# An MLP in two phases with its activations spilled to DRAM, and the up projection of most pairs of feature blocks with seven products for eight

## The chip, the cores and the metric

The kernel runs on one core of a Trainium2 chip. The metric is the time of one execution on the device in microseconds (us).

## The reference

One step of a one-layer decoder: an RWKV-7 branch and an mLSTM branch run on the same projection, are merged by gates, go through an output projection and then a squared-ReLU MLP. Two sets of tokens, 1024 of a prompt (with 16 meta tokens ahead) and 8 x 8 of running sequences, share the weights; after the mixing stages 1088 token columns are left. The change touches the end of the merge, the output projection and the MLP:

```
merged = ga * (ya @ p_a) + gb * (yb @ p_b)
h = x + rms_norm(merged @ w_out, post1)
u2 = rms_norm(h, pre2)
f = square(relu(u2 @ w_ff_up)) @ w_ff_down      # 1024 -> 4096 -> 1024
out = h + rms_norm(f, post2)
```

## The kernel before

All large products are made in float32 accuracy from three matmuls: an operand is split into a high part (`hi`, rounded) and a low part (`lo`, the rest), and `gemm` issues hi x hi, hi x lo and lo x hi into one PSUM bank (lines L219, L220, L221). Weights are loaded by `wload`: one DMA of 512 KB on SyncE's queue (L195), a cast on ScalarE (`hi`, L200) and subtractions on GpSimd (`lo`, L207) or VectorE (L203). Each of two pools (`wps`) holds one raw tile and two pairs of split ones, so weights come about one group ahead.

The merge (L1555 to L1568) makes `mg`, the 1088 token columns for 8 blocks of 128 rows, high and low part: for each of the 8 blocks it loads a row of gates (`gb`) and of the other branch (`pa`), multiplies on TensorE with p_b, and combines on VectorE (L1564), GpSimd (L1565), ScalarE (L1566) and VectorE (L1567). `wo_gemm` then multiplies with w_out, 8 blocks of 128 tokens and a ninth of 64 (the samples); for the ninth, high and low part stand side by side in one 128-column operand (`mgt`), two matmuls for three, except at k = 6. `pre_turn` transposes the normed result (L1606) back into `mg` (L1609, L1610).

The MLP works in 15 groups of f, blocks of 128 of the 4096 hidden features: three f, 13 times two, three f. For each group `up` makes the hidden rows of each f: three token tiles (`O_TILES`: 384, 384 and 320 columns) x 8 blocks k x 3 matmuls, then Relu (ScalarE, L1710), square (VectorE, L1711), cast (ScalarE, L1712) and subtraction (VectorE, L1716) into `AHS[f % 3]`. `down` then multiplies, for each of 8 blocks of tokens and both halves of the 1024 outputs, 3 matmuls of 512 columns per f, adds the bank to `ACC` on VectorE (L1771), and `down_tail` (L1735) does the ninth block. Up and down alternate, so only two or three f of hidden rows exist at a time, in SBUF. The first group's up is woven with the last three transposes (`todo`); the last group's down part is woven with the final norm and the outputs by hand (`manual_schedule`); elsewhere a scheduler sets the order of each engine's instructions from the program.

Of the kernel before, what the change touches and what calls it, by code (L numbers as in the profile page):

```python
# [8 lines left out]
F32 = mybir.dt.float32  # L9
# [8 lines left out]
D = 1024  # L18
# [84 lines left out]
def tile_hybrid_trunk_step(ctx, tc, x_prompt, x_sample, st_S, st_shift, st_C, st_n, st_m, st_conv,  # L103
# [58 lines left out]
    NKK = cp.tile([128, 4], F32, name="NKK")  # L162
    OKA = cp.tile([128, 4], F32, name="OKA")
# [1389 lines left out]
    for m in range(8):  # L1553
# [7 lines left out]
        for a, n in O_TILES:  # L1561
# [37 lines left out]
    def pre_turn(i, un_):  # L1599
        n, un = BL[i][1], un_.pop(i)  # L1600
        ts_ = slice(128 * i, 128 * i + n)
        for h in range(2):
# [5 lines left out]
            uh = mg[:, 0, 4 * h:4 * h + 4, ts_]  # L1608
            nc.scalar.copy(out=uh, in_=pv)  # L1609
            V.tensor_tensor(out=mg[:, 1, 4 * h:4 * h + 4, ts_], in0=pv, in1=uh.bitcast(F32), op=ALU.subtract)  # L1610
# [251 lines left out]
```

## Time and profile before

| | |
|---|---|
| median of 3 runs | 2058.99 us (2058.14 to 2061.21) |
| profiled execution | 2053.6 us, of which the span of the trace 2051.8 us |
| granted TensorE clock over the span | 0.987 of full speed |
| TensorE busy | 1943.2 us (95%), 12,325 matmuls in the trace |
| weight loads (PEld) | 1762.7 us (86%) |
| VectorE, ScalarE, GpSimd busy | 1266.4 (62%), 729.1 (36%), 589.4 us (29%) |
| DMA | 161.63 MB, 24.6% of the 16 engines' span |

A busy share is an average over stages with different limits; the MLP takes the last 790 of the 2052 us. Matmuls are pipelined: their durations overlap, and what one costs is the distance from its start to the next start.

### The profile page before, as it was taken

What the parts mean: (1) busy time and instruction counts of PE and PEld (TensorE: products, weight loads), DVE (VectorE), ACT (ScalarE), POOL (GpSimd) and SP (SyncE); (2) the same over time, 40 slices, a digit from 0 to 9 for tenths busy, and PEclk for the clock granted to TensorE, in tenths of its full rate; (3) what the DMA queues carried; (4) which work ended last, traced back from release to release, by engine and by line L of the source; (5) the groups of instructions that cost most, each with busy time, mean ns of one, the idle gap of its engine ahead of it and who ended that gap; (6) DMA issues with size and microseconds to landing.
All of it is one profiled execution on the core that took longest, in us unless ns stands there. A gap on an engine that the chain in (4) does not pass through costs nothing.

```text
span 2051.8 us, 32757 instructions
## 1 busy us (share of the span) xinstructions
PE 1943.2 (95%) x12325; PEld 1762.7 (86%) x12325; DVE 1266.4 (62%) x3527; ACT 729.1 (36%) x1706; POOL 589.4 (29%) x937
## 2 busy tenths in 40 slices
PE   8999899999999999999899998999999999999996
PEld 8988788888888888989788777889999999988895
DVE  6378778867877887777765469244444444444447
ACT  6444344433443343546554234322222222211122
POOL 3321221322122121353435115133222322232225
PEclk9999999999999999999999999999999999999998
DMA  5222112112111221143756334111111111111114
GB/s 157 56 77 66 47 56 64 58 47 67 63 56 56 67 66 57 54 129 117 233 185 206 132 99 153 32 52 42 52 52 42 42 51 43 42 42 52 42 37 163
DMA packets 148495, 161.63 MB, mean 79 GB/s; under 512 B 20428, under 2 KB 121606, under 8 KB 148336
## 3 DMA queue, kind: packets, MB, share of 16 engines
q1 hardware_dynamic: 148336, 159.54, 24.6%
q8 instruction: 97, 1.59, 0.3%
q14 instruction: 62, 0.51, 0.1%
HBM read 121.98 MB, written 37.27 MB: 78 GB/s over the span
## 4 chain that ended last, share of the span: by engine, by line
PE 63%; DVE 22%; DMA 7%; issue 3%; ACT 2%; POOL 1%; SPq 0%; DVEq 0%; ACTq 0%; POOLq 0%
PE g L219 11%; PE g L221 11%; PE g L220 11%; PE g L287 5%; PE g L283 5%; PE g L285 5%; DMA NR<-ndr 3%; DVE tmp L773 2%; DVE x L775 2%; DMA ndr<-nd 1%; PE g L1735 1%; DVE Vs L909 1%; PE a L713 1%; PE g L1635 1%; PE g L1637 1%
## 5 line engine op out<-in xcount | busy, mean ns | idle before, releaser
L207 POOL TENSOR_TENSOR lo<-raw,hi 128x128 fp32r<-128x128 f32 (+1 forms) x736 | 414.7, 596 | 985.8 <-ACT hi L200 971.6
L283 PE MATMUL g<-u,hi 128*128 128x414 f32 (+4 forms) x1120 | 379.8, 339 | 1.5 <-ACT hi L200 0.8
L287 PE MATMUL g<-u,lo 128*128 128x414 f32 (+4 forms) x1120 | 381.0, 340 | 0.0
L285 PE MATMUL g<-u,hi 128*128 128x414 f32 (+4 forms) x1120 | 378.9, 338 | 0.0
L200 ACT CAST hi<-raw 128x1024 fp32r<-128x1024 f32 x124 | 128.6, 1048 | 379.3 <-PE g L1735 275.8
L219 PE MATMUL g<-mg,hi 128*128 128x384 f32 (+1 forms) x768 | 251.7, 328 | 0.6 <-ACT mg L1609 0.6
L220 PE MATMUL g<-mg,hi 128*128 128x384 f32 (+1 forms) x768 | 251.4, 327 | 0.3 <-DVE mg L1610 0.3
L221 PE MATMUL g<-mg,lo 128*128 128x384 f32 (+1 forms) x768 | 251.5, 328 | 0.0
L1771 DVE TENSOR_TENSOR ACC<-g,ACC 128x512 f32<-128x512 f32 x234 | 161.4, 690 | 129.5 <-PE g L221 123.4
L283 PEld LDWEIGHTS g<-u,hi 128*128 128x128 f32 x1120 | 214.1, 191 | 6.8 <-issue 1.5
L287 PEld LDWEIGHTS g<-u,lo 128*128 128x128 f32 x1120 | 213.8, 191 | 4.9 <-POOL lo L207 0.3
L285 PEld LDWEIGHTS g<-u,hi 128*128 128x128 f32 x1120 | 213.7, 191 | 3.7 <-issue 0.2
L219 PE MATMUL g<-hi,ah 128*128 128x512 f32 (+1 forms) x515 | 202.9, 394 | 0.0
L220 PE MATMUL g<-lo,ah 128*128 128x512 f32 (+1 forms) x515 | 202.7, 394 | 0.0
L221 PE MATMUL g<-hi,ah 128*128 128x512 f32 (+1 forms) x515 | 202.4, 393 | 0.0
L219 PEld LDWEIGHTS g<-mg,hi 128*128 128x128 f32 x768 | 144.1, 188 | 1.5 <-ACT mg L1609 0.9
L220 PEld LDWEIGHTS g<-mg,hi 128*128 128x128 f32 x768 | 144.2, 188 | 1.2 <-DVE mg L1610 0.5
L221 PEld LDWEIGHTS g<-mg,lo 128*128 128x128 f32 x768 | 144.2, 188 | 0.0
L221 PEld LDWEIGHTS g<-hi,ah 128*128 128x128 f32 x515 | 96.7, 188 | 22.9
L219 PEld LDWEIGHTS g<-hi,ah 128*128 128x128 f32 x515 | 96.6, 187 | 22.3
L220 PEld LDWEIGHTS g<-lo,ah 128*128 128x128 f32 x515 | 96.7, 188 | 22.0
L773 DVE TENSOR_TENSOR tmp<-NR,x 128x45 f32<-128x45 f32 (+4 forms) x360 | 82.5, 229 | 28.4 <-DMA NR<-ndr 21.1
(855 smaller groups left out, 3482.1 us busy)
## 6 DMA issues: line engine op xcount, KB each, us to landing
raw<-in_w_in_dram SPq DMA_DIRECT2D x44, 512.0 KB
raw<-in_w_ff_up_dram SPq DMA_DIRECT2D x32, 512.0 KB
raw<-in_w_ff_down_dram SPq DMA_DIRECT2D x32, 512.0 KB
NR<-ndr SPq DMA_DIRECT2D x24, 384.0 KB
gscr<-gst SPq DMA_DIRECT2D x16, 544.0 KB
xt<-in_x_prompt_dram SPq DMA_DIRECT2D x15, 512.0 KB
ga<-gscr SPq DMA_DIRECT2D x8, 544.0 KB
pscr<-ga SPq DMA_DIRECT2D x8, 544.0 KB
```

Of the source, the lines that this page charges most:

```text
L200: nc.scalar.copy(out=hi, in_=raw)
L207: PO.tensor_tensor(out=lo[:, k:k + step], in0=raw[:, k:k + step], in1=hi[:, k:k + step].bitcast(F32), op=ALU.subtract)
L219: mm(ps, lhsT=wh, rhs=xh, start=(i == 0), stop=False)
L220: mm(ps, lhsT=wh, rhs=xl, start=False, stop=False)
L221: mm(ps, lhsT=wl, rhs=xh, start=False, stop=(i == last))
L283: mm(ps, lhsT=hi[:, k], rhs=xh, start=(k == 0), stop=False)
L285: mm(ps, lhsT=hi[:, k], rhs=xl, start=False, stop=False)
L287: mm(ps, lhsT=lo[:, k], rhs=xh, start=False, stop=(k == 7))
L713: mm(ps[:, 192 * (c - c0):192 * (c - c0) + 192], lhsT=flat(bd["a"][:, c]), rhs=flat(KB[:, c]), start=True, stop=True)
L773: V.tensor_tensor(out=tmp[:, :, :n], in0=NR[:, s + 1:16, :, s].rearrange("p t c -> p c t"), in1=x[:, :, s:s + 1].broadcast_to([128, G, n]) ...
L775: V.tensor_tensor(out=x[:, :, s + 1:16], in0=x[:, :, s + 1:16], in1=tmp[:, :, :n], op=ALU.add)
L1771: V.tensor_tensor(out=ACC[:, i, cs], in0=ps, in1=ACC[:, i, cs], op=ALU.add)
```

## The change

The hidden rows no longer stay in SBUF: phase 1 makes all 32 f and writes them to DRAM tensors `hD[f]`, phase 2 reads them back (`h_load`: DMA, cast, subtraction, four casts of the 32 sample columns each) into four buffers `AHS[f % 4]` and runs `down` as before.

In phase 1 the f 0 to 5 (`NCONV`) are made as before, with the square on ScalarE. The other 26 are 13 pairs. For a pair the product is seen as 2 x 2 blocks: the two f, the two halves of the 1024 inputs (4 blocks k each), and two interleaved halves of the tokens; Strassen's form (with shared sums) makes seven products in place of eight. A product is 2 quarters of the tokens (`q`) x 4 k x 3 matmuls of 272 columns. Products 1, 2 and 3 read `mg` itself, where the 272 columns are two runs of 136; products 5, 6, 7 and 4 read token sums T1 to T4, built once by `t_quads` on VectorE (28 operations of 128x1088) and ScalarE (8 casts). On the weight side `pair_prep` makes four sums S on VectorE and seven operands (cast on ScalarE, subtraction on GpSimd). `pair` puts the products together: two copies on ScalarE and 14 additions from PSUM on VectorE, then Relu and Square on ScalarE (128x1088, two of each) and four writes to `hD`.

So that a block of tokens has one size, `mg` is laid out in 8 blocks of 136 columns (128 of the prompt and 8 samples); the merge writes its last token tile in two pieces, and the ninth block of `wo_gemm` is stacked at k = 6 too. The seven products have eight PSUM banks instead of five. The last group's hand-written order is the same.

```diff
+            e = min(a + n, 1024)
+            parts = [(gb[:, a:e].rearrange("p (b c) -> p b c", c=128), [mgb[:, y, m, a // 128:e // 128, :128] for y in range(2)])]
+            if e < a + n:
+                parts.append((gb[:, 1024:].rearrange("p (b c) -> p b c", c=8), [mgb[:, y, m, :, 128:] for y in range(2)]))
+            for src, (mh, ml) in parts:
+                act(out=mh, in_=src, func=AF.Copy, scale=0.5)
+                V.scalar_tensor_tensor(out=ml, in0=src, scalar=0.5, in1=mh.bitcast(F32), op0=ALU.mult, op1=ALU.subtract)
...
-                    if i == 8 and k != 6:
-                        st_ = mgt[2][:, 0] if k == 4 else mgt[0][:, k] if k < 3 else mgt[1][:, k // 2 - 1]
+                    if i == 8:
+                        st_ = mgt[2][:, k // 2 - 2] if k in (4, 6) else mgt[0][:, k] if k < 3 else mgt[1][:, k // 2 - 1]
                         mm(ps, lhsT=st_, rhs=wh_, start=(k == 0), stop=False)
...
+    hD = [dp.tile([128, TO], F32, name=f"hD{f}") for f in range(32)]
+    HALF = [slice(0, 512), slice(512, 1024)]
+    NCONV = 6
+    PORDER = (1, 2, 6, 5, 7, 3, 4)
...
+            r_ = tmp()[:, :n]
+            act(out=r_, in_=ps, func=AF.Relu)
+            act(out=r_, in_=r_, func=AF.Square)
+            dma(out=hD[f][:, a:a + n], in_=r_)
...
+    for n in (4, 3, 1, 2):
+        phX[n] = ctx.enter_context(ExitStack())
+        T[n] = phX[n].enter_context(tc.tile_pool(name=f"tp{n}", bufs=1, side="right")).tile([128, 2, 4, TO // 2], F32R, name=f"T{n}")
...
+    def t_quads(q):
+        B = lambda j, l, y: mgb[:, y, 4 * j:4 * j + 4, 4 * q + l:4 * q + 4:2, :].bitcast(F32)
+        Tv = lambda n, y: T[n][:, y, :, HQ2 * q:HQ2 * q + HQ2].rearrange("p k (u c) -> p k u c", c=136)
+        fa, fb = [htile().rearrange("p k (u c) -> p k u c", c=136) for _ in range(2)]
+
+        def tt(o, x, y, op=ALU.subtract):
+            V.tensor_tensor(out=o, in0=x, in1=y, op=op)
+
+        def diff(b1, b2):
+            tt(fa, B(*b1, 0), B(*b2, 0))
+            tt(fb, B(*b1, 1), B(*b2, 1))
+            tt(fa, fa, fb, ALU.add)
+
+        def rest(o, b1, x):
+            tt(o, B(*b1, 0), x)
+            tt(o, o, B(*b1, 1), ALU.add)
+
+        def fin_(n, x):
+            nc.scalar.copy(out=Tv(n, 0), in_=x)
+            tt(Tv(n, 1), x, Tv(n, 0).bitcast(F32))
+
+        diff((0, 1), (0, 0))
+        rest(fb, (1, 1), fa)
+        fin_(1, fa)
+        rest(fa, (1, 0), fb)
+        fin_(2, fb)
+        fin_(4, fa)
+        diff((1, 1), (0, 1))
+        fin_(3, fa)
...
+    def operand(src):
+        o = slots[0]
+        slots[0] += 1
+        t_ = wps[o % 2].tile([128, 2, 4, 128], F32R, tag=("hi", "lo")[o // 2 % 2], name="op")
+        nc.scalar.copy(out=t_[:, 0], in_=src)
+        PO.tensor_tensor(out=t_[:, 1], in0=src, in1=t_[:, 0].bitcast(F32), op=ALU.subtract)
+        return t_
...
+    def pair_prep(p):
+        A = pair_load(p)
+        S = [stile() for _ in range(4)]
+        ops = {1: operand(A[0][0]), 2: operand(A[0][1])}
+        V.tensor_tensor(out=S[0], in0=A[1][0], in1=A[1][1], op=ALU.add)
+        V.tensor_tensor(out=S[1], in0=S[0], in1=A[0][0], op=ALU.subtract)
+        ops[6] = operand(S[1])
+        ops[5] = operand(S[0])
+        V.tensor_tensor(out=S[2], in0=A[0][0], in1=A[1][0], op=ALU.subtract)
+        ops[7] = operand(S[2])
+        V.tensor_tensor(out=S[3], in0=A[0][1], in1=S[1], op=ALU.subtract)
+        ops[3] = operand(S[3])
+        ops[4] = operand(A[1][1])
+        return ops
...
+    def Bop(n, y, k, q):
+        if n in (1, 2, 3):
+            j, l = ((0, 0), (1, 0), (1, 1))[n - 1]
+            return mgb[:, y, 4 * j + k, 4 * q + l:4 * q + 4:2, :]
+        return T[{5: 1, 6: 2, 7: 3, 4: 4}[n]][:, y, k, HQ2 * q:HQ2 * q + HQ2].rearrange("p (u c) -> p u c", c=136)
+
+    def prod(n, op, ps, q):
+        o = ps.rearrange("p (u c) -> p u c", c=136)
+        for k in range(4):
+            xh, xl = Bop(n, 0, k, q), Bop(n, 1, k, q)
+            mm(o, lhsT=op[:, 0, k], rhs=xh, start=(k == 0), stop=False)
+            mm(o, lhsT=op[:, 0, k], rhs=xl, start=False, stop=False)
+            mm(o, lhsT=op[:, 1, k], rhs=xh, start=False, stop=(k == 3))
+
+    def pair(p, ops):
+        X, H = {}, {}
+        add = lambda o, ps, x: V.tensor_tensor(out=o, in0=ps, in1=x, op=ALU.add)
+        for n in PORDER:
+            for q in range(2):
+                ps = gbank()[:, :HQ2]
+                prod(n, ops[n], ps, q)
+                if n == 1:
+                    X[q] = upp.tile([128, HQ2], F32, tag="X", name="X", bufs=4)
+                    H[q] = htile()
+                    nc.scalar.copy(out=X[q], in_=ps)
+                    continue
+                c11, c12, c21, c22 = [H[q][:, i] for i in range(4)]
+                if n == 2:
+                    add(c11, ps, X[q])
+                elif n == 6:
+                    add(X[q], ps, X[q])
+                elif n == 5:
+                    add(c12, ps, X[q])
+                elif n == 7:
+                    add(c22, ps, c12)
+                    add(c21, ps, X[q])
+                elif n == 3:
+                    add(c12, ps, c12)
+                elif n == 4:
+                    add(c21, ps, c21)
+                    act(out=H[q], in_=H[q], func=AF.Relu)
+                    act(out=H[q], in_=H[q], func=AF.Square)
+                    for i in range(2):
+                        dma(out=hD[2 * p + i][:, 2 * HQ2 * q:2 * HQ2 * q + 2 * HQ2], in_=H[q][:, 2 * i:2 * i + 2].rearrange("p s c -> p (s c)"))
+
+    for q in range(2):
+        t_quads(q)
+    for f in range(3, NCONV):
+        w, w3 = w3, up_load(f + 1) if f + 1 < NCONV else None
+        up(f, w, O_TILES, t1)
+    ops = pair_prep(NCONV // 2)
+    for p in range(NCONV // 2, 16):
+        nxt = pair_prep(p + 1) if p < 15 else None
+        pair(p, ops)
+        ops = nxt
...
+    hraw = lambda: dn.tile([128, TO], F32, tag="hr", name="hr", bufs=2)
+    AHS = [dn.tile([128, 2 * TO + 128], F32R, name=f"ah{i}") for i in range(4)]
...
+    def h_load(f):
+        ah, hr = AHS[f % 4], hraw()
+        dma(out=hr, in_=hD[f])
+        hi, lo, st_ = ah[:, :TO], ah[:, TO:2 * TO], ah[:, 2 * TO:]
+        nc.scalar.copy(out=hi, in_=hr)
+        V.tensor_tensor(out=lo, in0=hr, in1=hi.bitcast(F32), op=ALU.subtract)
+        for y, src in enumerate((hi, lo)):
+            for q in range(2):
+                v = src[:, 544 * q:544 * q + 544]
+                v = v.rearrange("p (u s c) -> p u s c", u=2, s=2) if f < NCONV else v.rearrange("p (s u c) -> p u s c", u=2, s=2)
+                nc.scalar.copy(out=st_[:, 64 * y + 32 * q:64 * y + 32 * q + 32].rearrange("p (u s c) -> p u s c", u=2, s=2),
+                               in_=v[:, :, :, 128:].bitcast(F32))
...
-    V.memset(SS, 1.0)
     for g, fs in enumerate(groups):
-        wu = [wload(kxm(w_ff_up[0], 128 * f, 128), 8, 128) for f in fs]
+        for f in fs:
+            h_load(f)
         if g == 0:
-            todo = [5,None,None,6,7]
```

On TensorE, a steady group of before passes from the up projection (`mg` against `hi`/`lo` of the weights) to the down projection (`ah` against the split down weights):

```order
L219 MATMUL g<-mg,hi 128x320
L220 MATMUL g<-mg,hi 128x320
L221 MATMUL g<-mg,lo 128x320
L219 MATMUL g<-hi,ah_13552 128x512
L220 MATMUL g<-lo,ah_13552 128x512
L221 MATMUL g<-hi,ah_13552 128x512
```

It is so in every group. After the change, a place in pair 10 (the second half of its 48 matmuls on `mg` for products 1 and 2 ends, product 6 on T2, `T_14800`, begins; `op` are the split weight operands, L1836 to L1838 the three matmuls):

```order
L1836 MATMUL g<-mg,op 128x272
L1837 MATMUL g<-mg,op 128x272
L1838 MATMUL g<-mg,op 128x272
L1836 MATMUL g<-T_14800,op 128x272 [waits DVE_49,Activation_49]
L1837 MATMUL g<-T_14800,op 128x272
L1838 MATMUL g<-T_14800,op 128x272 [waits Pool_49]
```

For each f stood 72 matmuls of 384 and 320 columns; for two f now stand 168 of 272, and no down projection stands between the pairs.

On SyncE's queue, where the loads of before alternate between up and down weights, a group ahead, at the change from phase 1 to phase 2 stand (`hD<-H` are writes of the last two pairs, `hr<-hD` the loads of f = 0, 1, 2, `raw` the down weights):

```order
L1869 DMA hD_14420<-H 128x544 [waits DMAHW5_49,Activation_49]
L1869 DMA hD_14421<-H 128x544 [waits DMAHW6_49,DVE_49]
L195 DMA raw<-in_w_ff_down_dram 128x1024 [waits DMAHW7_49,Activation_49,Pool_49]
L195 DMA raw<-in_w_ff_down_dram 128x1024 [waits DMAHW0_49,Pool_49]
L1899 DMA hr<-hD_14392 128x1088 [waits DMAHW1_49,PE_49]
L1899 DMA hr<-hD_14393 128x1088 [waits DMAHW2_49]
L195 DMA raw<-in_w_ff_down_dram 128x1024 [waits DMAHW3_49,DMAHW7_49,Activation_49,Pool_49]
L1899 DMA hr<-hD_14394 128x1088 [waits DMAHW4_49,DMAHW1_49,DVE_49]
L1869 DMA hD_14422<-H 128x544 [waits DMAHW5_49,Activation_49]
L1869 DMA hD_14423<-H 128x544 [waits DMAHW6_49]
L1869 DMA hD_14422<-H 128x544 [waits Activation_49]
L1869 DMA hD_14423<-H 128x544 [waits DMAHW0_49,DVE_49]
```

The loads of hidden rows are in the queue between weights and the last pair's writes; the first waits for TensorE, the third for VectorE.

On ScalarE at the same place (f = 0 is `ah_18289`, f = 1 `ah_18290`, f = 2 `ah_18291`; L1866 and L1867 are Relu and Square of pair 15):

```order
L1901 CAST ah_18289<-hr 128x1088 [waits DMAHW1_49]
L1866 ACTIVATE H<-H 128x1088 [waits DMAHW4_49,DMAHW3_49,DVE_49]
L1907 CAST ah_18289<-ah_18289 128x32 [waits Activation_49]
L1867 ACTIVATE H<-H 128x1088 [waits Activation_49]
L1866 ACTIVATE H<-H 128x1088 [waits DMAHW6_49,DMAHW5_49,DVE_49]
L1907 CAST ah_18289<-ah_18289 128x32
L1867 ACTIVATE H<-H 128x1088 [waits Activation_49]
L1907 CAST ah_18289<-ah_18289 128x32 x2
L1901 CAST ah_18290<-hr 128x1088 [waits DMAHW2_49]
L1901 CAST ah_18291<-hr 128x1088 [waits DMAHW4_49]
```

The cast of f = 0 stands ahead of pair 15's Relu and Square, those of f = 1 and 2 behind them.

On TensorE the last matmul of pair 15 is followed by 21 matmuls on f = 0, and these end so:

```order
L221 MATMUL g<-hi,ah_18289 128x512
L219 MATMUL g<-hi,ah_18290 128x512 [waits Activation_49]
L220 MATMUL g<-lo,ah_18290 128x512 [waits Pool_49]
L219 MATMUL g<-hi,ah_18290 128x512
L220 MATMUL g<-lo,ah_18290 128x512 [waits Pool_49]
L219 MATMUL g<-hi,ah_18290 128x512
L220 MATMUL g<-lo,ah_18290 128x512
L221 MATMUL g<-hi,ah_18290 128x512 [waits DVE_49]
L219 MATMUL g<-hi,ah_18291 128x512 [waits Activation_49]
```

Seven banks of group 0 are begun with f = 0 alone before f = 1 is asked for, and f = 2 is asked for 7 matmuls later.

## Rows read from the trace of the kernel before

**Rows 1.** Stretches: busy us of each engine (instructions), granted clock, DMA share, GB/s.

```profile
1260.00:1310.00 50.00, 48.12 (x279) 45.10 (x278) 32.51 (x64) 19.55 (x37) 18.79 (x23) 1.00 0.29 94
1400.00:1500.00 100.00, 100.00 (x520) 90.64 (x519) 41.40 (x67) 20.43 (x34) 27.08 (x45) 1.00 0.15 45
2000.00:2052.00 52.00, 33.68 (x155) 27.68 (x153) 41.02 (x77) 13.49 (x39) 28.20 (x20) 0.86 0.44 165
```

**Rows 2.** TensorE's waits, 1255 to 2052 us: total us, times, longest. Five rows.

```profile
PE s L1606 <- DVE SS L1589: 1.2, 1, 1.2
...
PE g L220 <- DVE mg L1610: 0.3, 1, 0.3
```

**Rows 3.** Timeline of TensorE, one steady group: start us, duration us.

```profile
1480.95 0.34 PE L219 MATMUL g<-mg,hi 128*128 128x384 f32 x1
1481.12 0.34 PE L220 MATMUL g<-mg,hi 128*128 128x384 f32 x1
...
1504.67 0.31 PE L221 MATMUL g<-mg,lo 128*128 128x320 f32 x1
1504.82 0.39 PE L219 MATMUL g<-hi,ah 128*128 128x512 f32 x1
...
1528.78 0.39 PE L1735 MATMUL g<-lo,ah 128*128 128x512 f32 x1
1529.01 0.34 PE L219 MATMUL g<-mg,hi 128*128 128x384 f32 x1
```

**Rows 4.** Timeline of TensorE: end of the first up part, last matmul.

```profile
1300.49 0.40 PE L219 MATMUL g<-hi,ah 128*128 128x512 f32 x1
...
2033.41 0.27 PE L221 MATMUL g<-hi,ah 128*128 128x192 f32 x1
```

**Rows 5.** Timeline of TensorE in the projection: two runs, 6 intervals of 276 columns each.

```profile
306.10 0.29 PE L283 MATMUL g<-u,hi 128*128 128x276 f32 x1
...
306.85 0.29 PE L283 MATMUL g<-u,hi 128*128 128x276 f32 x1
...
308.45 0.29 PE L287 MATMUL g<-u,lo 128*128 128x276 f32 x1
...
309.21 0.29 PE L287 MATMUL g<-u,lo 128*128 128x276 f32 x1
```

**Rows 6.** Groups by line and form: count, busy us, mean ns, idle before.

```profile
L219 PEld LDWEIGHTS g<-mg,hi 128*128 128x128 f32 x768 | 144.1, 188 | 1.5 <-ACT mg L1609 0.9
L1771 DVE TENSOR_TENSOR ACC<-g,ACC 128x512 f32<-128x512 f32 x234 | 161.4, 690 | 129.5 <-PE g L221 123.4 <-PE g L1735 6.1
L1564 DVE SCALAR_TENSOR_TENSOR gb<-gb,g 128x384 f32<-128x384 f32 x16 | 8.4, 546 | 4.4 <-DMA gb<-gscr 4.4
L207 POOL TENSOR_TENSOR lo<-raw,hi 128x128 fp32r<-128x128 f32 x672 | 332.1, 528 | 713.0 <-ACT hi L200 698.8 <-ACT R L252 11.6 <-issue 1.6
L207 POOL TENSOR_TENSOR lo<-raw,hi 128x512 fp32r<-128x512 f32 x64 | 82.7, 1316 | 272.8 <-ACT hi L200 272.8
L1609 ACT CAST mg<-s 128x512 fp32r<-128x512 f32 x16 | 8.8, 586 | 5.4 <-PE s L1606 5.4
L200 ACT CAST hi<-raw 128x1024 fp32r<-128x1024 f32 x124 | 128.6, 1048 | 379.3 <-PE g L1735 275.8 <-PE g L220 48.0 <-PE g L285 17.8
```

**Rows 7.** Timeline of GpSimd, then of VectorE, near 1295 us.

```profile
1294.68 2.80 POOL L207 TENSOR_TENSOR lo<-raw,hi 128x512 fp32r<-128x512 f32 x2 [20.16 <-ACT hi L200]
...
1294.91 1.41 DVE L1711 TENSOR_TENSOR r__14667<-r__14667 128x320 f32<-128x320 f32 x1 [2.51 <-ACT r__14667 L1710]
```

**Rows 8.** Single lines: duration min/median/max ns, first and last start us.

```profile
L1415 DVE TENSOR_TENSOR yh<-yt,yh x2: 1292/1292/1293, 1001.6 to 1074.9; 128x1088 fp32r<-128x1088 f32 x2
...
L1414 ACT CAST yh<-yt x3: 1087/1099/1100, 1000.5 to 1073.8; 128x1088 fp32r<-128x1088 f32 x3
...
L1610 DVE TENSOR_TENSOR mg<-s,mg x18: 411/682/690, 1222.6 to 1286.8; 128x512 fp32r<-128x512 f32 x16, 128x256 fp32r<-128x256 f32 x2
```

**Rows 9.** Chain that ended last, in the merge: start us, us, what.

```profile
1100.87 4.71 DMA gb<-gscr
```

More of the change, by code (lines that the diff above doesn't have):

```diff
@@ L1607, in pre_turn @@
             pv = pt.rearrange("p (k t) -> p k t", k=4)[:, :, :n]
-            uh = mg[:, 0, 4 * h:4 * h + 4, ts_]
+            ks = slice(4 * h, 4 * h + 4)
+            uh, ul = [mgb[:, y, ks, i, :128] if i < 8 else mgb[:, y, ks, :, 128:] for y in range(2)]
+            if i == 8:
+                pv = pv.rearrange("p k (b c) -> p k b c", c=8)
             nc.scalar.copy(out=uh, in_=pv)
-            V.tensor_tensor(out=mg[:, 1, 4 * h:4 * h + 4, ts_], in0=pv, in1=uh.bitcast(F32), op=ALU.subtract)
+            V.tensor_tensor(out=ul, in0=pv, in1=uh.bitcast(F32), op=ALU.subtract)
     SS = sm.tile([128, 11, 2], F32, tag="SS", name="SS", bufs=1)
@@ L1718, in tile_hybrid_trunk_step, with up_load @@
-    gam3 = gam1
-    dma(out=gam3, in_=post2.broadcast_to([128, D]))
-    HALF = [slice(0, 512), slice(512, 1024)]
+            r_ = tmp()[:, :n]
+            act(out=r_, in_=ps, func=AF.Relu)
+            act(out=r_, in_=r_, func=AF.Square)
+            dma(out=hD[f][:, a:a + n], in_=r_)
+    def up_load(f):
+        return wload(kxm(w_ff_up[0], 128 * f, 128), 8, 128)
+    t1 = lambda: rpool.tile([128, 384], F32, tag="r_", name="r_")
+    wu = [up_load(f) for f in range(3)]
+    todo = [5, None, None, 6, 7]
@@ new lines, in tile_hybrid_trunk_step @@
+    for tile_ in O_TILES[:2]:
+        for f, w in enumerate(wu):
+            up(f, w, (tile_,), t1)
+            for i in todo[:1]:
+                if i:
+                    pre_turn(i, un_)
+            todo = todo[1:]
+    w3 = up_load(3)
+    for f, w in enumerate(wu):
+        up(f, w, O_TILES[2:], t1)
+    phN.close()
+    phS.close()
+    gps3 = ctx.enter_context(tc.tile_pool(name="gps3", bufs=3, space=PSUM))
+    gpss[:] = (gps, gps2, gps3, gps2, gps3, gps, gps2, gps3)
+    phT = ctx.enter_context(ExitStack())
@@ new lines, in tile_hybrid_trunk_step, with pair_load @@
+    slots = [0]
+    def operand(src):
[5 more added lines that the diff above has]
+        return t_
+    def pair_load(p):
+        srcs = [kxm(w_ff_up[0], 256 * p + 128 * i, 128) for i in range(2)]
+        if p % 2:
+            t_ = raw2()
+            tiles = [t_[:, i] for i in range(2)]
+        else:
+            tiles = [wps[i].tile([128, 8, 128], F32, tag="raw", name="raw", bufs=1) for i in range(2)]
+        for t_, src in zip(tiles, srcs):
+            dma(out=t_, in_=src)
+        return [[t_[:, 4 * j:4 * j + 4] for j in range(2)] for t_ in tiles]
@@ new lines, in tile_hybrid_trunk_step, with at_ @@
+    AHS = [dn.tile([128, 2 * TO + 128], F32R, name=f"ah{i}") for i in range(4)]
+    late.close()
+    phT.close()
+    phB.close()
+    fin = ctx.enter_context(tc.tile_pool(name="fin2", bufs=1))
+    ACC = fin.tile([128, 9, D], F32, name="ACC2")
+    gam3 = fin.tile([128, D], F32, name="gam3")
+    sm = ctx.enter_context(tc.tile_pool(name="sm2", bufs=2))
+    def at_(f, i):
+        return 136 * i if f < NCONV else 544 * (i // 4) + 272 * (i % 2) + 136 * (i // 2 % 2)
+    def h_load(f):
[10 more added lines that the diff above has]
+                               in_=v[:, :, :, 128:].bitcast(F32))
```

83 lines of the change are left out of this document (36 added, 47 removed).

## The prediction

> **What bounds the kernel now.** I read the table of stretches first. In the MLP's steady part TensorE is busy all of 100 us, at a granted clock of 1.00, while VectorE is busy 41, ScalarE 20 and GpSimd 27, and the DMA engines move 45 GB/s; only the last 52 us are otherwise (0.86, TensorE busy 33.7) [rows 1]. The list of waits says the same of the whole MLP: from 1255 us on TensorE waited five times, the longest 1.2 us, the shortest 0.3 [rows 2]. So in this stage one column less through TensorE is time off the kernel, and work on the other engines is free until one of them makes TensorE wait.
>
> A busy TensorE is pipelined, so durations (0.31 to 0.39 us) are no prices; spacings are. In one steady group [rows 3] the starts of two 384-column matmuls lie 0.17 us apart, of two 320-column ones 0.15 and of two 512-column ones 0.23; the up projection of two f runs from 1480.95 to 1504.82, 23.87 us, and the down projection on to 1529.01, 24.19 us. The up part of the first group, three f, ends at 1300.49; the last matmul of the kernel starts at 2033.41 [rows 4]. Per f and column tile there are 24 matmuls, so one f is 24 x (384+384+320) = 26,112 columns in 11.935 us: 0.457 ns per column.
>
> **The change, part by part.** *Fewer matmuls.* For 26 of 32 f the up projection goes from 72 matmuls (11.935 us) to half of a pair's 7 x 2 x 4 x 3 = 168 matmuls of 272 columns. No row has 272, but the projection at the start has 276: six spacings take 0.75 us from 306.10 to 306.85 and 0.76 from 308.45 to 309.21 [rows 5], 0.125 to 0.127 each, or 0.453 to 0.459 ns per column. I take 272 x 0.4555 = 0.1239 us (bounds 0.1232 to 0.1257, the last if the shorter matmul costs all that 276 does). A pair is then 168 x 0.1239 = 20.8 us instead of 23.87, and 13 pairs 270.6 instead of 310.3: **-39.7 us** (-35.8 to -41.2). In products 1, 2 and 3 the moving operand consists of two runs of 136 columns apart from each other; no row shows such a read. I price it as one run; the bound above is a rival.
>
> The rows show no constant per matmul: 276 columns cost as much per column as 512. The Trainium skill, "TensorE: Matmul & The Clock Gate", section "Back-to-back issue gap", gives an isolated gap of N/2.4 + 2.5 ns, which has one. By it (an estimate) 512 columns would take 0.216, not 0.23, and shorter matmuls would lose by their number: 26 x 24 x (0.1625 + 0.1625 + 0.1358) = 287.6 against 2,184 x 0.1158 = 253.0, a gain of 34.7 us. The trace differs from its figures, so the rows decide.
>
> *Work that the other engines gain, per pair of 20.8 us.* VectorE: 14 additions from PSUM of 272 columns, which have no row, at 0.42 us by the line through 0.55 at 384 columns and 0.69 at 512 (nothing and 0.55 are the bounds), and four weight sums of 512, 0.69 each as the nearest row [rows 6]: 8.6 us. A 320-column VectorE operation on two operands in SBUF took 1.41 us under two subtractions of GpSimd (1294.68 to 1297.48) [rows 7], where 384 columns take 0.55; additions from PSUM ran beside such work in every group, and their 234 took 0.69 on average [rows 6]. Only the four sums can be hit, so 8.6 + 4 x 1.1 = 13 is my upper bound. ScalarE: 7 casts of 512 (0.59), two copies, and Relu and Square of 1088 columns twice (1.10, [rows 8]): 9.3 us. GpSimd: 7 subtractions of 512 (1.32): 9.2 us. None reaches 20.8. DMA: 1.05 MB of weights and 1.1 MB of hidden rows out, 2.1 MB in 20.8 us or 103 GB/s; a load of 0.54 MB landed in 4.71 us [rows 9]. The operands have eight slots for seven in use, so an operand is cast when the product six or seven places ahead of it ended, some 17 us early. The sharpest wait inside is the H tile: the second product's additions of a pair need the write of the pair before to have left it. After the last product that is an addition, Relu, Square and a landing: 0.4 + 2 x 2.2 + 4.7 = 9.5 us behind TensorE, and the bank that waits for it is needed again 8 tiles of 1.49 us after its use, at some 15 to 16 us. Five us are left, so I cost it at nothing.
>
> *The token sums.* 28 VectorE operations of 1088 columns at 1.29, 36 us, begin when the last transposed block is split, 1286.8 [rows 8], and end at about 1323. GpSimd splits three weights of the up projection in that time (three times 8 x 0.53, [rows 6]: 13 us); at the ratio of [rows 7] VectorE gets 5 us of work done in those 13, so 1331 is nearer. What covers them is the conventional f 3 to 5: these begin at 1300.5 and take 35.8, so the first product on a sum (6, after products 1 and 2) is due at 1336.3 + 5.95 = 1342. Cost nothing; without that cover it would be the 36 us themselves.
>
> *Stacked rows of block 8.* Twice one 512-column matmul less: -0.5 us. *The pieces of mg in the merge.* Eight more operations each on ScalarE and VectorE, 64 columns, beside a chain that goes through such loads there [rows 9]; and SyncE issues the p_b weights ahead of the first pa and gb. I take +1 (bounds -1 to +3).
>
> *From up to down.* Before, up and down of each group alternate and both weights are a group ahead. Now, as the orders of SyncE, ScalarE and TensorE show, the spilled rows come back through T's space: the load of f=0 waits for product 7 of the last pair, which ends 5.95 us before TensorE is through (call that end E). Landing 4.7, cast 1.1: high part at E, low part (1.29) at E+1.4. On ScalarE the Relu and Square of the last pair (4.4 us, waiting for an addition behind that low part) stand ahead of the cast of f=1, so its parts come at about E+5.5 and E+7; the load of f=2 waits for f=0's low part, lands at E+6 and its low part comes at E+9.5. TensorE does 21 matmuls of f=0 first (4.9 us), then 7 of f=1, then needs f=2. Stall 1.4 + about 1.6: **+3 us** (1.5 to 12, the last if every load is issued one landing later). *Group 0 to 1:* f=4 takes the buffer of f=0 and its weights the slot of wd 0, free only when group 0 is done; a cast and a low part (1.05 to 1.10, 1.3) follow, and only four matmuls of f=3 (0.9) lie before: **+2.5** (1 to 5). *Before f=31* the same for its weights: **+1** (0 to 2). Elsewhere in the second phase rows and weights are one group ahead: 2.1 MB per 24.2 us (87 GB/s), VectorE 18 x 0.69 + 2 x 1.29 = 15.0 and ScalarE 2 x (1.10 + 1.05) and eight small casts, under 8, of 24.2 [rows 6]. The down matmuls and the tail after 2033.41 (18.4 us) are the same instructions: 0 (±2).
>
> **Sum.** -39.7 - 0.5 + 1 + 3 + 2.5 + 1 = -32.7 us, against the profiled execution of 2053.6 us (span 2051.8 and 1.8 around it): 2020.9. That execution is 5.4 us below the median of the runs shown, so against the median 2058.99 - 32.7 = **2026.3 us**. Adding up the bounds gives -41.2 - 0.5 - 1 + 1.5 + 1 + 0 - 2 = -42 and -35.8 - 0.5 + 3 + 12 + 5 + 2 + 2 = -12; the ends together are unlikely.
>
> **Rivals.** *(A) The seams cost more.* Each of the three places where a group finds its rows or weights late can cost a whole load, cast and subtraction, 4.7 + 1.1 + 1.3 = 7 us, instead of the 1 to 3 above; and a TensorE that stands still there may be granted its lower clock for some us afterwards, as in the last 52 us (0.86). Three times 7 and 3 to 5 for the clock is 25 where I have 6.5: 2058.99 - 32.7 + 18 = 2044. For it: every load stands on one SyncE queue behind writes that wait. Against: 45 GB/s leave the DMA engines idle, and the waits of [rows 2], up to 1.2 us, left the clock at 1.00 between 1260 and 1310 [rows 1].
>
> *(B) Weight loads set a floor (slower than before).* Every matmul loads 128 columns of weights; the load's row says 0.188 us [rows 6], more than 0.124. If loads did not overlap, 2,184 x 0.188 = 410.6 us stand against 310.3: +100, 2126 us with the seams. It decides as soon as a matmul of 272 costs over (310.3 - 7) / 2,184 = 0.139 us. Against: the 276-column rows load as many weights and are spaced 0.126. What is left for it is the split moving operand of products 1 to 3: 936 matmuls; at 0.188 for these alone +60 us, 2086. Only a spacing below 0.124 + 32.7 / 936 = 0.159 there keeps the kernel faster.
>
> *(C) An engine becomes the bound inside a pair.* If H's write lands 12 us after its issue and not 4.7, the bank is late by 1 to 2 us in each pair, and operands that come late with it may add as much: 22 to 23.9 us a pair instead of 20.8, 13 x 1.2 to 3.1 us, so 2042 to 2067. Against: the five us and the half-idle engines above.
>
> *(D) The seams hide.* If the merge gains 1 and the seams cost their lower bound, 2.5 in all: 2058.99 - 39.7 - 0.5 - 1 + 2.5 = 2020; with the lower bound per column 2018.5.
>
> **Chances.** The forecast 0.64 (its own range 2019 to 2035), A 0.16, C 0.08, B 0.06, D 0.06. The range reaches from D's edge to A: 2017 to 2045, which leaves out B, most of C and a part of A, under 2 in 10. Runs of before differ by 3 us, so 0.2% (4 us) is about what a measurement can tell from no change: faster 0.90 (forecast, A, D and half of C), same 0.03, slower 0.07.
>
> **What would show each step.** Spacings of 0.124 us at 272 columns, alike on T and on mg; pairs 20.8 us apart without TensorE waits; product 6 of the first pair not waiting for VectorE; waits of 1 to 4 us on the first ah rows, on f=4 and on f=31's weights, and nowhere else; down groups of 24.2 us. I am wrong if TensorE's spacing on mg differs from that on T, if VectorE or ScalarE releases it inside the pairs, or if the granted clock drops at E.

## The result and the profile after

The changed kernel takes 2027.07 us (median of 4 runs, 2019.21 to 2031.76), before 2058.77 (4 runs): a ratio of 0.984, 95% interval 0.981 to 0.987. The forecast was 2026.3. The profiled execution of the change took 2031.76 us (span 2030.0, mean clock 0.980), that is 4.7 us above its median, where the one of before was below its own; so the two traces differ by 21.8 us and the medians by 31.7. Where these ten come from is the first reading.

Granted clock and engines from 800 to 900 us, long before the change, of the changed kernel and then of a version with one buffer more in phase 2 (columns as in [rows 1]):

```profile
800.00:900.00 100.00, 94.78 (x576) 89.75 (x573) 63.60 (x159) 40.49 (x71) 33.68 (x53) 0.90 0.23 72
...
800.00:900.00 100.00, 94.34 (x583) 89.41 (x582) 69.11 (x171) 45.53 (x81) 39.70 (x55) 0.95 0.29 90
```

TensorE's order is the same in these two up to the output projection, and yet this stretch is granted 0.90 in one execution and 0.95 in the other; the second version, traced once more, has 0.90 as well. So it isn't the program that makes the difference, and what does is not shown. The first matmul of the output projection stands at 1147.87 us in the trace of before, at 1154.88 in the changed kernel's, and between 1143.8 and 1156.3 in five traces of the changed kernel and its variants. So I count from that matmul on: before 2051.8 - 1147.87 = 903.9 us, after 2030.0 - 1154.88 = 875.1: **-28.8 us**. A second trace of the changed kernel has 2026.0 - 1150.84 = 875.2, so from there on the traces agree. From the first p_b matmul of the merge on, which the change touches as well (1089.32 and 1097.42), it is -29.9.

Stretches of the changed kernel, a piece of the pairs and the change of phase (columns as in [rows 1]):

```profile
1400.00:1500.00 100.00, 100.00 (x799) 100.00 (x798) 37.08 (x84) 43.51 (x64) 42.86 (x34) 1.00 0.33 104
1620.00:1626.00 6.00, 3.44 (x15) 2.44 (x13) 1.29 (x1) 2.11 (x3) 0.76 (x1) 1.00 1.00 315
1626.00:1630.00 4.00, 3.84 (x10) 3.09 (x11) 1.37 (x2) 2.19 (x11) 0.00 (x0) 0.57 1.01 362
```

In the pairs TensorE is busy all of 100 us, and so is the weight loader (100.00 where [rows 1] had 90.64, an average of up and down projection). That is nothing new in the pairs. In the kernel before, in an up projection of 384 and 320 columns, the loader is busy throughout as well:

```profile
1481.00:1504.60 23.60, 23.60 (x144) 23.60 (x143) 7.15 (x12) 7.37 (x13) 8.85 (x12) 1.00 0.23 68
```

A load's row is 0.188 us long [rows 6] and the matmuls are closer than that in both, so the rows of the loads overlap and their share says little about whether they set the pace. At the change of phase there is a hole: 3.44 of 6 us busy, and then four microseconds at a granted clock of 0.57. TensorE's waits from 1290 us to the end (total, times, longest) are these alone:

```profile
PE g L219 <- ACT ah L1901: 2.7, 1, 2.7
PE g L220 <- POOL lo L207: 0.8, 2, 0.6
PE g L221 <- DVE ah L1902: 0.2, 1, 0.2
```

The timeline of TensorE shows the pairs: the start of pair 3 at 1342.15, and of a later pair product 1 at 1405.41, product 6, product 3, and product 1 of the next (`mg` is the token operand itself, `T` a sum):

```profile
1342.15 0.29 PE L1836 MATMUL g<-mg,op 128*128 128x272 f32 x1
...
1405.41 0.29 PE L1836 MATMUL g<-mg,op 128*128 128x272 f32 x1
...
1411.42 0.29 PE L1836 MATMUL g<-T,op 128*128 128x272 f32 x1
...
1420.47 0.29 PE L1836 MATMUL g<-mg,op 128*128 128x272 f32 x1
...
1426.50 0.29 PE L1836 MATMUL g<-mg,op 128*128 128x272 f32 x1
```

From the product on mg at 1405.41 to the same one of the next pair at 1426.50 it is 21.09 us; 1342.15 + 13 x 21.09 is 1616.3, where phase 2 begins. 48 matmuls on mg take 1411.42 - 1405.41 = 6.01 us, 72 on T 9.05: 0.1252 and 0.1257 us each, so reading two runs of 136 costs nothing.

The change of phase and the end, TensorE's timeline again (f = 0 at 1616.28; group 1 begins at 1657.46, group 2 at 1682.88, the last matmul is at 2010.22):

```profile
1616.28 0.40 PE L219 MATMUL g<-hi,ah 128*128 128x512 f32 x1
...
1617.15 0.50 PE L221 MATMUL g<-hi,ah 128*128 128x512 f32 x1 [0.25 <-DVE ah L1902]
...
1626.16 0.80 PE L219 MATMUL g<-hi,ah 128*128 128x512 f32 x1 [2.72 <-ACT ah L1901]
1626.75 0.63 PE L220 MATMUL g<-lo,ah 128*128 128x512 f32 x1
1627.18 0.63 PE L221 MATMUL g<-hi,ah 128*128 128x512 f32 x1
...
1657.46 0.40 PE L219 MATMUL g<-hi,ah 128*128 128x512 f32 x1
...
1682.88 0.40 PE L219 MATMUL g<-hi,ah 128*128 128x512 f32 x1
...
2010.22 0.27 PE L221 MATMUL g<-hi,ah 128*128 128x192 f32 x1
```

The stretches side by side, in us of TensorE's starts:

| stretch | before | after | difference |
|---|---|---|---|
| output projection to first up matmul | 111.36 | 110.91 | -0.5 |
| six f by the conventional way | 41.26 + 35.8 | 76.36 | -0.7 |
| the other 26 f | 310.3 | 274.13 | -36.2 |
| down, group 0 | 36.28 | 41.18 | +4.9 |
| down, group 1 | 24.2 | 25.42 | +1.2 |
| last group and tail | 54.5 | 56.7 | +2.2 |

The twelve groups between take 24.2 us in both. The sum is -29.1, within rounding of the 28.8 above.

### The profile page after: what moved, and what is told of

Read it like the earlier page. It is cut to its first block, busy times and chain, and to the rows that moved or that the text cites. A ratio compares the mean times of both kernels' runs of the same rounds, so it can differ in the third digit from the quotient of the medians.

```text
span 2030.0 us, 34260 instructions
## 1 busy us (share of the span) xinstructions
PE 1918.5 (95%) x12635; PEld 1737.2 (86%) x12635; DVE 1332.9 (66%) x3604; ACT 804.6 (40%) x1869; POOL 624.7 (31%) x820
## 5 line engine op out<-in xcount | busy, mean ns | idle before, releaser
L207 POOL TENSOR_TENSOR lo<-raw,hi 128x128 fp32r<-128x128 f32 (+1 forms) x528 | 330.7, 661 | 786.2 <-ACT hi L200 733.4
L200 ACT CAST hi<-raw 128x1024 fp32r<-128x1024 f32 x98 | 102.7, 1049 | 68.5 <-PE g L285 17.8
L1901 ACT CAST ah<-hr 128x1088 fp32r<-128x1088 f32 x32 | 34.0, 1103 | 221.7 <-PE g L220 217.8
L1838 PE MATMUL g<-T,op 128*128 128x272 f32 x416 | 120.1, 289 | 0.0
L1836 PE MATMUL g<-T,op 128*128 128x272 f32 x416 | 120.1, 289 | 0.0
L1837 PE MATMUL g<-T,op 128*128 128x272 f32 x416 | 119.9, 288 | 0.0
L1797 POOL TENSOR_TENSOR op<-S,op 128x512 fp32r<-128x512 f32 x52 | 68.4, 1316 | 82.8 <-ACT op L1796 81.1
L1838 PE MATMUL g<-mg,op 128*128 128x272 f32 x312 | 89.8, 288 | 0.0
```

Of the source, the lines that this page charges most:

```text
L200: nc.scalar.copy(out=hi, in_=raw)
L207: PO.tensor_tensor(out=lo[:, k:k + step], in0=raw[:, k:k + step], in1=hi[:, k:k + step].bitcast(F32), op=ALU.subtract)
L1836: mm(o, lhsT=op[:, 0, k], rhs=xh, start=(k == 0), stop=False)
L1837: mm(o, lhsT=op[:, 0, k], rhs=xl, start=False, stop=False)
L1838: mm(o, lhsT=op[:, 1, k], rhs=xh, start=False, stop=(k == 3))
```

## The experiments

**What a matmul of 272 columns costs.** The pairs save 36.2 us, not 39.7: a matmul costs 0.1255 us, not 0.1239. Is that a price by columns, or does the weight loader, busy throughout, set a floor? In three runs 154 of the 168 matmuls of a pair were made narrower (256, 208 and 144 columns; the sums for the other columns of each product are left out):

```diff
+        o2 = ps[:, :256].rearrange("p (u c) -> p u c", c=128)
         for k in range(4):
-            mm(o, lhsT=op[:, 0, k], rhs=xh, start=(k == 0), stop=False)
+            mm(o if k == 0 else o2, lhsT=op[:, 0, k], rhs=xh if k == 0 else xh[:, :, :128], start=(k == 0), stop=False)
...
```

> Of the 168 matmuls of a pair 154 work on 256 columns in place of 272 (the other 16 columns of each product are left wrong). Theory A (a matmul costs its columns, 0.4545 ns each): spacing 0.116 us, a pair 19.97 us in place of 21.09, 14.6 us less in all: 2012 us. Theory B (the weight load of 128 columns sets a floor of 0.1255 us, and 272 columns lie on it): spacing and pairs unchanged, 2027 us.

> The same with 208 columns (64 columns of each product left wrong). Theory A (columns): spacing 0.0945 us, a pair 16.6 us, 58 us less: 1969 us. Theory B (floor by the weight load): spacing 0.125 us, 21.1 us a pair, 2027 us.

> 154 of the 168 matmuls of a pair on 144 columns (128 columns of each product left wrong). At 256 columns a pair took 20.05 us and at 208 18.96, so a matmul 0.1188 and 0.1117 us. Theory (a line of 0.447 ns per column and 4 ns above a floor of about 0.111 us): still 0.111 us a matmul, 18.9 us a pair. Rival (no floor, only a flatter line below 256 columns, 0.15 ns per column): 0.102 us, 17.5 us a pair. Rival (columns alone): 0.068 us, 12.3 us a pair, if no other engine stops it.

Timelines of TensorE: the first matmul of product 3 of one pair and of the next, with 256 columns:

```profile
1410.57 0.29 PE L1837 MATMUL g<-mg,op 128*128 128x272 f32 x1
...
1430.62 0.29 PE L1837 MATMUL g<-mg,op 128*128 128x272 f32 x1
```

with 208, product 1:

```profile
1413.18 0.30 PE L1837 MATMUL g<-mg,op 128*128 128x272 f32 x1
...
1432.13 0.30 PE L1837 MATMUL g<-mg,op 128*128 128x272 f32 x1
```

with 144, product 1:

```profile
1409.64 0.33 PE L1837 MATMUL g<-mg,op 128*128 128x272 f32 x1
...
1428.59 0.33 PE L1837 MATMUL g<-mg,op 128*128 128x272 f32 x1
```

A pair takes 20.05, 18.95 and 18.95 us, and TensorE waits for nothing inside the pairs of these three. With 14 matmuls left, taken at 0.1255, the others cost (20.05 - 1.76) / 154 = 0.1188, 0.1116 and 0.1116 us. The times were 2010.5, 2006.6 and 1998.4 us (the last a single run). So both theories hold a part, and at 208 columns neither had the number: down to 256 columns a line decides, and at 208 and 144 there is a floor of 0.112 us, which the line would reach at some 240 columns (an estimate). The line through 512 columns (104 matmuls in 24.19 us, [rows 3]: 0.2326) and 272 (0.1255) is 0.446 ns per column and 4 ns for each matmul; it gives 0.1184 at 256 and 23.90 us for the up part that took 23.87 in [rows 3]. That what makes the floor is the weight load is not shown apart: every matmul here loads 128 columns of weights, and none was tried with fewer. By the Trainium skill, "TensorE: Matmul & The Clock Gate", section "LDWEIGHTS (loading the stationary operand)", the load of 128 columns takes 128 / 1.2 = 107 ns (an estimate by the page's formula). The measured floor is 5 ns above that.

**The spill without the products.**

```diff
-    NCONV = 6
+    NCONV = 32
-    for q in range(2):
-        t_quads(q)
-    ops = pair_prep(NCONV // 2)
-    for p in range(NCONV // 2, 16):
...
```

> All 32 f by the conventional up projection, but still in two phases through DRAM: the spill alone, without the seven products. Theory (the gain is the columns taken from TensorE, the seams cost some us): the 36.2 us that 13 pairs saved in the trace come back, 2027 + 36 = 2063 us, about 4 us slower than before, with the same waits at the change of phase. Rival (the seams cost nothing, or the split into phases itself saves something): 2059 us or less.

Measured: 2057.3 us, ratio to before 0.9994 (0.9970 to 1.0017). The rival holds: two phases and the round trip through DRAM cost nothing that can be told (the interval is some 5 us to either side), so the gain comes from the products. Its TensorE timeline, first up matmul, the change of phase, group 1 and the last matmul:

```profile
1260.73 0.42 PE L219 MATMUL g<-mg,hi 128*128 128x384 f32 x1
...
1645.23 0.31 PE L221 MATMUL g<-mg,lo 128*128 128x320 f32 x1
1645.38 0.39 PE L219 MATMUL g<-hi,ah 128*128 128x512 f32 x1
...
1681.61 0.40 PE L219 MATMUL g<-hi,ah 128*128 128x512 f32 x1
...
2033.41 0.27 PE L221 MATMUL g<-hi,ah 128*128 128x192 f32 x1
```

Up passes to down without a hole (1645.23, 1645.38), group 0 takes 36.2 us as before, and from the first up matmul to the last one it is 772.7 us where before it was 774.2 (1259.23 to 2033.41). So the hole of the changed kernel is not the price of spilling as such. But the seam is another one here: no token sums stand in the space for the rows that come back, and SyncE issues the first of their loads 346 us ahead of the first down matmul:

```profile
1299.62 0.45 SPq L1892 DMA_DIRECT2D hr<-hD  x1
```

In the changed kernel the first of these loads waits for TensorE in the last pair and goes out at 1610.45, 6 us ahead.

**The hole at the change of phase.** SyncE, ScalarE and VectorE of the changed kernel there, and last SyncE's own waits from 1616 to 1618.9 us:

```profile
1610.45 0.80 SPq L1899 DMA_DIRECT2D hr<-hD  x2
1618.27 0.33 SPq L195 DMA_DIRECT2D raw<-in_w_ff_down_dram  x1
1618.70 0.37 SPq L1899 DMA_DIRECT2D hr<-hD  x1
1619.17 3.06 SPq L1869 DMA_DIRECT2D hD<-H  x4
...
1620.01 1.11 ACT L1901 CAST ah<-hr 128x1088 fp32r<-128x1088 f32 x1
1625.01 1.10 ACT L1901 CAST ah<-hr 128x1088 fp32r<-128x1088 f32 x1 [3.89 <-DMA hr<-hD]
...
1615.60 1.49 DVE L1902 TENSOR_TENSOR ah<-hr,ah 128x1088 fp32r<-128x1088 f32 x1 [0.19 <-ACT ah L1901]
...
SPq L195 <- POOL lo L207: 3.6, 1, 3.6
```

Two loads of hidden rows are issued at 1610.45, early enough; the third, f = 2, at 1618.70. It needs the buffer `hr` that the low part of f = 0 reads until 1617.09; but what it waits for last is its place in the queue, behind a load of down weights that itself waits 3.6 us for a subtraction on GpSimd and goes out at 1618.27. It lands at 1625.0, in a stretch in which the DMA engines are all busy (1620 to 1626: share 1.00). ScalarE's cast begins at 1625.01, and TensorE, which waited for it, at 1626.16. The experiment gives that load a third buffer:

```diff
-    hraw = lambda: dn.tile([128, TO], F32, tag="hr", name="hr", bufs=2)
+    hraw = lambda: dn.tile([128, TO], F32, tag="hr", name="hr", bufs=3)
```

> Three buffers for the rows that come back (hr) instead of two, so that the load of f=2 doesn't wait for the low part of f=0. Theory (that load, issued 1618.7 and landed 1625.0, is what TensorE waits for): the wait of 2.7 us at the change of phase falls under 1 us and the granted clock stays at 1.00 behind it: 3 to 4 us less, 2023 us. Rival (ScalarE's order, the Relu and Square of the last pair ahead of the casts, sets the wait; or the load lands late behind the down weights anyway): the wait stays at 2 us or more, 2027 us.

Timelines of SyncE, ScalarE and TensorE:

```profile
1603.73 1.27 SPq L1899 DMA_DIRECT2D hr<-hD  x3
...
1613.28 2.10 ACT L1901 CAST ah<-hr 128x1088 fp32r<-128x1088 f32 x2
...
1609.56 0.40 PE L219 MATMUL g<-hi,ah 128*128 128x512 f32 x1
...
1610.42 0.50 PE L221 MATMUL g<-hi,ah 128*128 128x512 f32 x1 [0.24 <-DVE ah L1902]
...
1646.27 0.40 PE L219 MATMUL g<-hi,ah 128*128 128x512 f32 x1
```

All three loads are issued by 1605.0, now ahead of that load of weights (1611.55 here), the casts of f = 1 and 2 run back to back at 1613.28, and only the 0.24 us for the low part of f = 0 are left. Group 0 takes 1646.27 - 1609.56 = 36.7 us where it took 41.2, and no stretch there has a clock under 1.00. The buffer and the new place in the queue came together; a run with the order alone was not made. The time was 2021.3 us (ratio 0.984, 0.980 to 0.987). Three more runs: that version with a fourth tile for S (and two tiles for X in place of four), the changed kernel again, and beside it the version with three hr buffers again:

> The same with NCONV = 6: three hr buffers and four S tiles. Theory: the sums are covered anyway, so the fourth S tile changes nothing and the time is that of the three hr buffers, 2022.5 us. Rival (the S waits cost TensorE time in the pairs): 2 us or more below that.

> The changed kernel itself once more, beside the version with three hr buffers. Both theories: 2027 us, with the wait of 2.7 us at the change of phase and a lower granted clock for some 3 us behind it.

> Three hr buffers, on the same chip as the changed kernel. Theory (the late load of f=2 and the clock behind it are worth 4.5 us): 4 to 5 us less than the changed kernel beside it, 2022.5 us. Rival (the trace's gain is lost in the runs, or another wait takes its place): within 2 us of it.

The version with four S tiles took 2022.4 us (ratio 0.985, 0.983 to 0.987), the changed kernel again 2026.7 (0.984, 0.982 to 0.986), the three hr buffers again 2025.2 (0.984, 0.982 to 0.986). From the first matmul of phase 2 to the end of the span the two traces of the changed kernel show 413.7 and 413.7 us (1616.28 to 2030.0, 1612.34 to 2026.0), the three with three hr buffers 409.6, 409.5 and 409.6. The mended hole is worth 4.1 us in every trace, and it is not to be told in the medians, whose runs scatter over 10 us, in the traces ahead of the output projection. Beside each other the two medians differ by 1.5 us, which by what I expected is the rival's result. I call the version better in that stretch, and its total unproven. The fourth S tile changes nothing: the 13 pairs take 274.13 us with it, as without.

**The cover of the token sums.**

```diff
-    NCONV = 6
+    NCONV = 4
```

> NCONV = 4: one more pair by seven products (2.8 us less on TensorE), and 23.9 us less of conventional work to cover the token sums. Theory (the sums need the cover): in the trace T2's second half is ready at 1334.5, 42 us after the sums begin, and now it is due at about 1326, so TensorE waits for VectorE some 8 us at product 6 of the first pair: 2027 - 2.8 + 8 = 2032 us. Rival (VectorE's waits inside the sums, 6.4 us for an operand, go away with the cover and the sums are ready in time): 2024 us and no wait at product 6.

```diff
-    NCONV = 6
+    NCONV = 4
-    stile = lambda: upp.tile([128, 4, 128], F32, tag="S", name="S", bufs=3)
+    stile = lambda: upp.tile([128, 4, 128], F32, tag="S", name="S", bufs=4)
...
-                    X[q] = upp.tile([128, HQ2], F32, tag="X", name="X", bufs=4)
+                    X[q] = upp.tile([128, HQ2], F32, tag="X", name="X", bufs=2)
...
-    hraw = lambda: dn.tile([128, TO], F32, tag="hr", name="hr", bufs=2)
+    hraw = lambda: dn.tile([128, TO], F32, tag="hr", name="hr", bufs=3)
```

> A version meant to be better: three hr buffers, NCONV = 4, and four S tiles (X cut to two) so that VectorE doesn't wait for GpSimd inside the token sums. Theory: the change of phase gives 4.5 us as before, the extra pair 2.8, and product 6 of the first pair waits 0 to 4 us: 2020 to 2024 us. Rival (the sums can't be ready): a wait of 8 us or more there, 2028.

Measured: 2038.2 us (0.992, 0.989 to 0.995), and with the other three edits 2041.8 (0.993, 0.990 to 0.996). In the first of the two TensorE waits 11.4 us in the first pair (5.7 for VectorE's part of T, 5.7 for ScalarE's), and is granted less than its full clock meanwhile and behind it:

```profile
1320.00:1330.00 10.00, 3.77 (x15) 3.46 (x16) 10.00 (x6) 3.33 (x5) 7.31 (x4) 0.62 0.23 69
1330.00:1340.00 10.00, 6.51 (x38) 6.09 (x38) 9.97 (x11) 2.43 (x4) 3.75 (x2) 0.84 0.00 0
```

The 14 pairs take 1622.63 - 1310.62 = 312.0 us instead of 274.13 x 14 / 13 = 295.2: 16.8 lost, 11.4 of them waiting; the rest I put down to the clock. The theory was right and too small. A part of why the sums take so long is on VectorE's rows, and then GpSimd's:

```profile
1292.64 1.28 DVE L1766 TENSOR_TENSOR H<-H,mg 128x1088 f32<-128x1088 f32 x1
...
1312.88 1.28 DVE L1766 TENSOR_TENSOR T<-H,T 128x1088 fp32r<-128x1088 f32 x1
...
1324.43 2.35 DVE L1766 TENSOR_TENSOR T<-H,T 128x1088 fp32r<-128x1088 f32 x1
...
1326.70 2.36 DVE L1766 TENSOR_TENSOR H<-H,mg 128x1088 f32<-128x1088 f32 x1
...
1292.53 7.95 POOL L1797 TENSOR_TENSOR op<-raw,op 128x512 fp32r<-128x512 f32 x1 [19.46 <-PE g L221]
1300.45 1.29 POOL L1797 TENSOR_TENSOR op<-S,op 128x512 fp32r<-128x512 f32 x1
...
1325.59 2.32 POOL L1797 TENSOR_TENSOR op<-S,op 128x512 fp32r<-128x512 f32 x1
```

The same VectorE operation takes 1.28 us or 2.35, and a GpSimd subtraction 1.29, 2.32 or 7.95. Alone each takes its short time (VectorE at 1312.88, GpSimd at 1300.45). Beside each other either both take about 2.3 us (1325.59 and 1326.70), or VectorE keeps its 1.28 (1292.64) and GpSimd takes 7.95. Which of the two comes, and why, no run here separates. Six of the 28 sums were slowed in this way, by about a microsecond each; ten weight sums of the first pairs stand among them on VectorE as well. The fourth S tile, with two X tiles, did not help (waits of 13.5 us).

In the changed kernel VectorE stands still in the middle of the sums, for an operand of GpSimd:

```profile
1318.34 0.69 DVE L1821 TENSOR_TENSOR S<-raw,S 128x512 f32<-128x512 f32 x1 [6.39 <-POOL op L1797]
```

**Can the write of a pair make TensorE wait?** VectorE of the changed kernel at a pair's beginning (product 1 of this pair begins at 1426.50, so product 2's first bank is written from 1429.51 on):

```profile
1433.22 0.44 DVE L1842 TENSOR_TENSOR H<-g,X 128x272 f32<-128x272 f32 x1 [6.07 <-DMA hD<-H]
```

The addition of product 2 waits 6.07 us for the write of the pair before, and is done at 1433.66. Its bank is asked for eight tiles later, at 1429.51 + 8 x 1.507 = 1441.57: 7.9 us are left. Four writes in place of one:

```diff
                     for i in range(2):
+                        dma(out=hE[2 * p + i][...], in_=H[q][...])
+                        dma(out=hF[2 * p + i][...], in_=H[q][...])
+                        dma(out=hG[2 * p + i][...], in_=H[q][...])
                         dma(out=hD[2 * p + i][...], in_=H[q][...])
```

> Each half of a pair's hidden rows is written four times (three copies to spare DRAM tensors), so that H leaves late. In the trace a write lands 4.8 us after its issue and the bank that waits for it is asked for 7.9 us after it is free. Theory (the trace's slack): TensorE waits only by what the last of the four writes lands later than 12.7 us after its issue; with 16 writes of 0.28 MB at about 300 GB/s that is some 14 to 15 us, so 1 to 2 us a pair: 2040 to 2053 us. Rival (five us of slack, as the prediction had): 4 to 5 us a pair, 2080 us. If writes overlap better than that: 2027.

```profile
1400.00:1500.00 100.00, 100.00 (x799) 100.00 (x798) 37.47 (x85) 43.26 (x64) 43.36 (x33) 1.00 0.75 258
```

The DMA engines move 258 GB/s in this stretch instead of 104, and TensorE doesn't wait: 799 matmuls in 100 us as before, 2025.8 us (0.986, 0.983 to 0.990). The 1 to 2 us a pair that I expected did not come. VectorE's order is another in this version: the addition of product 2 stands behind a weight sum that waits 10.66 us for GpSimd, and is done at 1418.29, 2.7 us before its bank is asked for (1421.01). So the transfers don't bound the pairs at two and a half times the traffic; how much the 7.9 us themselves can bear is not shown.

## Why the prediction was right, point by point

- **Fewer matmuls: mechanism right, size off.** -36.2 us for -39.7. The step that failed is "the rows show no constant per matmul": I took 276 columns at 0.125 to 0.127 for proportional to 512 and scaled to 272 with 0.4555 ns per column. The rows had a line with a constant in them: the up and the down part of [rows 3] together (23.87 us for 96 matmuls of 384 and 48 of 320 columns, 24.19 for 104 of 512) give 0.448 ns per column and 3.4 ns for each matmul, so 0.1252 us at 272 columns and a saving of 36.9. The 276-column spacings, read to 0.01 us over six intervals, could not tell it from no constant. And 2,184 matmuls in place of 1,872 pay it more often. The bound of -35.8 held. The Trainium skill, "TensorE: Matmul & The Clock Gate", section "Back-to-back issue gap", which I set aside, has such a constant. The estimate by it (34.7) was nearer than mine; its 2.4 columns per ns and 2.5 ns are not the measured ones (2.24 and 4).
- **Rival B, weight loads.** The loads overlap, and mg costs what T costs; the rival is out as priced. But a floor is there, 14 ns under the price of 272 columns. The 2126 us I gave for it adds its 100 to a forecast that has the saving in it already; with the seams it would have been 2166.
- **Engines in the pairs: right.** VectorE is busy 37 of 100 us, ScalarE 44, GpSimd 43; additions of 272 columns take 0.44 us (0.42 forecast). No wait inside the pairs; the slack behind the write is 7.9 us, not 5. Rival C is out.
- **Token sums: right that they hide, with less room than thought.** The last sum is done at 1343.3, and product 7, which reads it, is due at 1354.2 (four products of 3.01 us behind 1342.15), 11 us later. I had 1331 for the end, 1337.6 in a trace in which the up projection begins 6.6 us later; what I left out is that VectorE stands 6.4 us for an operand that GpSimd finishes late (until 1318.34). The price without cover, which I gave as 36 us, is 17 with one f of cover left.
- **From up to down: +4.9 for +3.** The waits were 0.25 and 2.72 us for 1.4 and 1.6, on the rows named; the rest, 1.9 us, is the clock, which I had only in rival A. A falling clock at this place was one of my signs of being wrong, and it came. That f = 2 would be last was right, and the version with three buffers shows it; but I had its load landing 6 us behind the end of the pairs, and it landed 8.7 behind, held back in the queue and 6.3 us on its way instead of 4.7.
- **Group 0 to 1: +1.2 for +2.5**, a wait of 0.62 us for the low part of the weights and slower starts about it. **Before f = 31**: a wait of 0.23 us; but the last group and the tail are 2.2 us longer where I had 1 and 0. The tail behind the last matmul is 19.8 us, and so it is in the version without products (18.4 before), so the products don't make it; its cause I didn't test.
- **Merge: -1.1 for +1** (58.55 and 57.46 us from the first p_b matmul to the output projection). But the same code takes 57.05 to 59.14 us in the traces of the other versions, so neither a cost nor a gain of the merge can be told from that scatter.
- **Sum.** -29.9 in the traces, -31.7 between medians, -32.7 forecast: the saving was 3.5 too large, the merge up to 2.1 too dear, and the seams, forecast at 6.5 and the tail at 0, came to 8.3 together. These errors cancel in part, and the runs of the change lie between 2019.2 and 2031.8: that forecast and median are 0.8 us apart is luck. What the traces bear out is the mechanism, and the size to about 3 us.

## What to carry to other kernels

Where TensorE is busy throughout, price a new matmul width from a line through at least two widths of the trace, since a constant of a few ns hides in any proportion, and don't take the weight loader's busy share for a sign of a floor: it was 100% at 384 and 320 columns as at 144. A change of phase can cost next to nothing if its first loads are issued in time: here three loads some 5 us ahead left a wait of 0.24 us, while two buffers left the third load behind a waiting one in the same queue, and the lower clock made the wait of 2.7 us dearer. When runs scatter by 10 us for a reason far from the change, compare traces from the last common instruction on.

## What was not expected of the hardware

- A wait of TensorE of 2.72 us, in a stretch with 3.44 of 6 us busy, was followed by a granted clock of 0.57 over the next 4 us, in which 512-column matmuls were spaced 0.43 us (1626.75 to 1627.18) and not 0.233: the lower of the two levels, 1.2 and not 2.4 GHz. It came again in the second trace of the changed kernel (a wait of 2.68 us, 0.57). The waits of up to 1.2 us in [rows 2] had cost nothing of the kind.
- Beside each other, VectorE operations with both operands in SBUF and GpSimd's subtractions took longer, but not always both: 1.28 us became up to 2.38 for 1088 columns on the one, 1.29 became up to 7.95 for 512 columns on the other, and in the longest case VectorE lost nothing. The 272-column additions from PSUM took 0.44 us throughout the pairs.
- Matmuls of 208 and of 144 columns cost the same, 0.112 us each, with a weight load of 128 columns for every one.
